# The input map of a state-space mixer as one float32r product over three stacked splits

## The chip, the cores and the metric

The kernel runs on one core of a Trainium2 chip. The metric is the device time of one execution in microseconds (us). The core's engines work side by side, each on its own list of instructions in a fixed order: TensorE (PE; its weight loads are listed as PEld), VectorE (DVE), ScalarE (ACT), GpSimd (POOL) and SyncE (SP), which here issues nearly all DMA transfers.

## The reference

A decoder of two layers over 256 positions with 2048 channels. Each layer has a hybrid mixer with four groups, a cross attention to a memory and a feed-forward network with 5632 hidden channels. The part that is changed is the input map of the first group, a state-space mixer with 32 groups of 16 channels and 64 complex states:

```python
bb_re = z_re[..., None] * b_re - z_im[..., None] * b_im
bb_im = z_re[..., None] * b_im + z_im[..., None] * b_re
bu_re = jnp.einsum('bsgc,gpc->bsgp', uf, bb_re)
bu_im = jnp.einsum('bsgc,gpc->bsgp', uf, bb_im)
...
_, _, x_re, x_im = lax.associative_scan(_s5_combine, elems, axis=1)
y = (jnp.einsum('bsgp,gcp->bsgc', x_re, c_re) - jnp.einsum('bsgp,gcp->bsgc', x_im, c_im)
     + d_skip * uf)
```

The factor `z` depends on group and state only. The recurrence between the two maps is linear with one coefficient for each group and state.

## The kernel before

Nearly all the work is products of the 256 positions with large weight matrices. Weights and activations are f32; each is split into a rounded float32r part (`whi`, `h`) and a remainder (`wlo`, `l`), and three float32r products stand for one. `load_split` brings a weight tile of 256 rows by 512 columns into one of three buffers `raw` (line 271, on SP's queue), ACT rounds it (line 272), DVE subtracts (line 273). There are four buffers for each result. Each tile then feeds twelve products of 512 columns (lines 285 to 287).

The small parts of a layer are written as generators ("lanes"). `pump`, called after each tile of a weight product, advances each lane by its rate, so their instructions are spread among the weight products. A planner then sets the order of instructions on each engine from this written order, from priorities (`load_split` stands 100 places earlier) and from when it takes operands and buffers to be ready. The order is fixed before the kernel runs.

The state-space lane has three parts. `s5_prep` runs once a layer (in layer 0 in the mixer's first block, in layer 1 during the feed-forward network before): it loads B and C, multiplies B by `z` on DVE (lines 604 to 610), transposes both on PE in sets of four (lines 613 and 626) and makes the tables `tab`. `s5_mixer` goes through four quarters `j` of four tiles `ii`. `u`, transposed to `uT`, is copied for each tile by POOL into 32 rows of `band`, whose other rows are zero (line 694), and two f32 products of 256 columns give the real and the imaginary input of the recurrence (lines 700 and 701). Some 14 DVE instructions for each tile do the recurrence (lines 704 to 723), then the output map `CT` is applied (line 730). `s5_tail` applies the gate and the norm and leaves the group's split result in `ys_h` and `ys_l`, which `w_out` needs last but one: it starts with the tiles of two other groups.

The pool `xt` (16 buffers of 4 KB a partition) holds activations, tables and maps; `k4` (7 buffers) holds attention operands.

Of the kernel before, what the change touches and what calls it, by code (L numbers as in the profile page):

```python
# [10 lines left out]
F = mybir.dt.float32  # L11
# [3 lines left out]
AF = mybir.ActivationFunctionType  # L15
OP = mybir.AluOpType
# [3 lines left out]
T = 256  # L20
D = 2048
L = 2
# [3 lines left out]
MAGIC = 12582912.0  # L26
ALPHA = (2 * L) ** 0.25
S5_RATE, CMP_RATE, NSA_RATE, SB_RATE, REST_RATE, PREP_RATE, XA_RATE = 1.05, 1.0, 0.9, 0.9, 2.0, 1.0, 1.3
N_K4, N_EV, N_S5, N_ATT, N_RAW, N_W, N_MM = 7, 3, 6, 7, 3, 4, 4
SPLIT_AHEAD = 100  # L30
FIRST_BLK = 4
N_Y4 = 1
# [6 lines left out]
TF = 128  # L39
# [2 lines left out]

_CONST_PARTS = [
    ("ident", 128), ("ropek", 128), ("ropeq", 128), ("ropec", 64), ("blk", 8), ("sel", 128),
    ("perm", 128), ("cmask", 32), ("cvalid", 2), ("mt", 256), ("ntri", 128), ("tio", TF), ("par", 2), ("sel4", 32),
]
_MASK_PARTS = [("causal", 128), ("strict", 128), ("dil", 256)]

# [1 line left out]
def _shape_consts():  # L50
    p = np.arange(128)
    c = {}
    c["ident"] = np.eye(128)
    inv = (np.float32(10000.0) ** (-np.arange(32, dtype=np.float32) / np.float32(32))).astype(np.float32)

    def tab(pos):
        a = (pos.astype(np.float32)[:, None] * inv[None, :]).astype(np.float32).astype(np.float64)
        return np.cos(a), np.sin(a)

    cs = np.zeros((128, 2, 2, 32))  # L60
    for tt in range(2):
# [24 lines left out]
    c["cmask"] = cm.reshape(128, 32)  # L86
    c["cvalid"] = cv
    d = p[:, None] + 128 - np.arange(256)[None, :]
    mt = (d >= 0) * ((d <= 128) * 1.0 + (d % 4 == 0) + (d % 16 == 0))
    c["mt"] = mt  # L90
    c["ntri"] = -1.0 * (p[:, None] >= p[None, :])
    c["tio"] = np.broadcast_to(np.arange(float(TF))[None, :], (128, TF))
    c["par"] = np.stack([(p // 16) % 2 == 0, (p // 16) % 2 == 1], 1)
    c["sel4"] = (p[:, None] % 32 == np.arange(32)[None, :])
    m = {}
    m["causal"] = np.where(p[None, :] <= p[:, None], 0.0, NEG)
    m["strict"] = np.where(p[:, None] < p[None, :], 0.0, NEG)
    m["dil"] = np.where(mt > 0, 0.0, NEG)
    f = [np.asarray(c[n], np.float32).reshape(128, w) for n, w in _CONST_PARTS]
    g = [np.asarray(m[n], np.float32).reshape(128, w) for n, w in _MASK_PARTS]  # L100
    return np.ascontiguousarray(np.concatenate(f + g, 1))


def bcast_rows(ap, n):
# [4 lines left out]
def kernel(ctx: ExitStack, tc: tile.TileContext, a: dict, cst: bass.AP, out: bass.AP,  # L109
# [3 lines left out]
    te, ve, ae, ge, sy = nc.tensor, nc.vector, nc.scalar, nc.gpsimd, nc.sync  # L113
# [22 lines left out]
    C, o = {}, 0  # L136
# [3 lines left out]
    ident = C["ident"]  # L140
# [20 lines left out]
    band = const.tile([128, 4, T], F, name="band")  # L161
    for t in (*pair, band):
        ge.memset(t, 0.0)
    turn_of_pair = [0]

# [14 lines left out]
    def ps(name="ps"):  # L180
        return psum.tile([128, 512], F, tag="ps", bufs=8 - N_MM, name=name)
# [23 lines left out]
        return wk.tile(list(shape), F, tag="y4", bufs=N_Y4, name=name)  # L205

    def xt_piece(name, shape=(128, 4, T), dt=R):
        return main.tile(list(shape), dt, tag="xt", bufs=16, name=name)

    def dump(key, ap):  # L210
        if key in dbg:
# [377 lines left out]

    def s5_prep(l, phi, zz, turn, res):  # L590

        BT = xt_piece("BT", (128, 2, 4, 128), F)
        CT = xt_piece("CT", (128, 2, 4, 128), F)
        bn = [s52([128, 16, 16], name="bn") for _ in range(2)]
        for q, n in enumerate(("s5_b_re", "s5_b_im")):
            v = a[n][l].rearrange("(i q) p c -> q p i c", q=2)
            for g in range(2):
                sy.dma_start(bn[q][g * 64:(g + 1) * 64], v[g])
        zr = zz[:, 0, l, :, None].to_broadcast([128, 16, 16])
        zi = zz[:, 1, l, :, None].to_broadcast([128, 16, 16])  # L600
        for q in range(2):
            t12 = s52([128, 2, 16, 16], name="bt")
            t1, t2 = t12[:, 0], t12[:, 1]
            ve.tensor_tensor(t1, bn[q], zr, op=OP.mult)
            ve.tensor_tensor(t2, bn[1 - q], zi, op=OP.mult)
            bx = s52([128, 16, 2, 16], name="bx")
            ge.memset(bx, 0.0)
            for g in range(2):
                s = slice(g * 64, (g + 1) * 64)
                ve.tensor_tensor(bx[s, :, g, :], t1[s], t2[s], op=OP.add if q else OP.subtract)  # L610
            pt = ps()
            for j in range(4):
                te.transpose(pt[:, j * 128:(j + 1) * 128],
                             bx[:, 4 * j:4 * j + 4].rearrange("p i q c -> p (i q c)"), ident)
            ae.activation(BT[:, q].rearrange("p j s -> p (j s)"), pt, AF.Copy)
            yield
        for q, n in enumerate(("s5_c_re", "s5_c_im")):
            cn = s52([128, 4, 64], name="cn")
            sy.dma_start(cn, a[n][l].rearrange("(j g) c p -> (g c) j p", g=8))
            ce = s52([128, 4, 2, 64], name="ce")  # L620
            for g in range(2):
                ve.tensor_scalar(ce[:, :, g, :], cn, C["par"][:, g:g + 1], -1.0 if q else 1.0,
                                 op0=OP.mult, op1=OP.mult)
            pt = ps()
            for j in range(4):
                te.transpose(pt[:, j * 128:(j + 1) * 128], ce[:, j].rearrange("p q s -> p (q s)"), ident)
            ae.activation(CT[:, q].rearrange("p j s -> p (j s)"), pt, AF.Copy)
            yield
        tabs = []
        res.update(BT=BT, CT=CT, tabs=tabs, turn=turn[l])  # L630
        for i4 in range(4):
            tb = xt_piece(f"tab{i4}", (128, 4, 2, TF), F)
            av = s52([128, 4, TF], name="ta")
            y = s52([128, 4, TF], name="ty")
            for i in range(4):
                ae.activation(y[:, i], C["tio"], AF.Copy, scale=phi[:, l, 4 * i4 + i:4 * i4 + i + 1])
            ve.tensor_scalar(av, y, MAGIC, -MAGIC, op0=OP.add, op1=OP.add)
            ve.tensor_tensor(y, y, av, op=OP.subtract)
            act(tb[:, :, 1, :], y, AF.Sin, scale=SIN_SCALE)
            ae.activation(av, y, AF.Abs)  # L640
            act(tb[:, :, 0, :], av, AF.Sin, scale=-SIN_SCALE, bias=halfpi)
            tabs.append(tb)
            yield
# [37 lines left out]
        yield  # L681

    def s5_mixer(l, u, prep, mag, out_y):
        BT, CT, tabs = prep["BT"], prep["CT"], prep["tabs"]
        uT = xt_piece("uT", dt=F)
        tcos, tsin = prep["turn"]
        for tt in range(2):
            nat_T(u[:, tt], uT, tt)
        yield
        for j in range(4):  # L690
            X = []
            for ii in range(4):
                rs = slice(ii * 32, ii * 32 + 32)
                ge.tensor_copy(band[rs, ii], uT[rs, j])
            for ii in range(4):
                i = 4 * j + ii
                tb = tabs[j][:, ii, :, None, :].to_broadcast([128, 2, 2, TF])
                fr = "p q (f t) -> p q f t"
                pb = ps("pb").rearrange("p (q t) -> p q t", q=2)
                te.matmul(pb[:, 0], BT[:, 0, j, :], band[:, ii], start=True, stop=False, skip_group_check=True)  # L700
                te.matmul(pb[:, 1], BT[:, 1, j, :], band[:, ii], start=False, stop=True, skip_group_check=True)
                A = s52([128, 2, T], name="rA")
                B = s52([128, 2, T], name="rB")
                ve.tensor_tensor(A.rearrange(fr, f=2), pb.rearrange(fr, f=2), tb, op=OP.mult)
# [586 lines left out]
    for l in range(layers):  # L1291
# [43 lines left out]
        prep_gen = None  # L1335


_INS = ["x", "mem", "ln_in_g", "ln_in_b", "w_in", "s5_lambda_re", "s5_lambda_im", "s5_log_dt", "s5_b_re", "s5_b_im",
        "s5_c_re", "s5_c_im", "s5_d", "s5_w_glu", "s5_b_glu", "nsa_cmp_pe", "nsa_cmp_w1", "nsa_cmp_w2", "mix_norm_g",
        "w_out", "ln1_g", "ln1_b", "xa_wq", "xa_wkv", "xa_wo", "ln2_g", "ln2_b", "ffn_w_gate", "ffn_w_up",  # L1340
        "ffn_w_down", "ln3_g", "ln3_b"]

# [19 lines left out]
```

## Time and profile before

| | |
|---|---|
| median of three runs | 2576.04 us (2575.46 to 2577.42) |
| the profiled execution | 2577.51 us, its span 2575.4 us |
| PE busy | 2521.7 us, 98% of the span |
| DVE busy | 1613.9 us, 63% |
| ACT busy | 1225.8 us, 48% |
| moved by DMA | 457.67 MB, 178 GB/s on average |
| granted TensorE clock | 0.998 of full speed on average |

The span runs from the first to the last instruction. Matmuls are pipelined: a record of one shows longer than the distance to the next, so this document takes distances between starts. An f32 product has two records.

### The profile page before, as it was taken

What the parts mean: (1) busy time and instruction counts of PE and PEld (TensorE: products, weight loads), DVE (VectorE), ACT (ScalarE), POOL (GpSimd) and SP (SyncE); (2) the same over time, 40 slices, a digit from 0 to 9 for tenths busy, and PEclk for the clock granted to TensorE, in tenths of its full rate; (3) what the DMA queues carried; (4) which work ended last, traced back from release to release, by engine and by line L of the source; (5) the groups of instructions that cost most, each with busy time, mean ns of one, the idle gap of its engine ahead of it and who ended that gap; (6) DMA issues with size and microseconds to landing.
All of it is one profiled execution on the core that took longest, in us unless ns stands there. A gap on an engine that the chain in (4) does not pass through costs nothing.

```text
span 2575.4 us, 32103 instructions
## 1 busy us (share of the span) xinstructions
PE 2521.7 (98%) x12019; PEld 2035.3 (79%) x12019; DVE 1613.9 (63%) x2378; ACT 1225.8 (48%) x1739; POOL 73.1 (3%) x137
## 2 busy tenths in 40 slices
PE   7999999999999999999999999999999999999997
PEld 5767778878888888888877777788788888888886
DVE  7887866676554554454679877675755555545546
ACT  3656584444434434434544567645444444344342
POOL 1000000000000000000000000100000000000000
PEclk9999999999999999999999999999999999999999
DMA  8644446556666666666656435465666666666664
GB/s 230 174 120 119 131 144 201 178 167 195 189 194 189 192 191 189 192 191 190 209 161 181 117 114 173 143 200 173 211 188 191 194 190 189 193 189 188 195 189 146
DMA packets 256027, 457.67 MB, mean 178 GB/s; under 512 B 25936, under 2 KB 38528, under 8 KB 255872
## 3 DMA queue, kind: packets, MB, share of 16 engines
q1 hardware_dynamic: 255296, 454.58, 59.6%
q8 instruction: 94, 1.54, 0.2%
q10 hardware_dynamic: 576, 1.05, 0.1%
q14 instruction: 61, 0.50, 0.1%
HBM read 453.47 MB, written 2.10 MB: 177 GB/s over the span
## 4 chain that ended last, share of the span: by engine, by line
PE 90%; DVE 5%; DMA 2%; ACT 1%; issue 1%; POOL 0%; SPq 0%; POOLq 0%; DVEq 0%; ACTq 0%
PE mm L287 25%; PE mm L285 25%; PE mm L286 25%; PE tr L377 2%; DVE wlo L273 2%; PE mm L311 1%; PE mm L313 1%; PE mm L312 1%; PE pt L813 1%; PE ns L932 1%; PE nY L946 1%; DVE H L415 1%; ACT whi L272 1%; PE pb L700 1%; PE nt L650 0%
## 5 line engine op out<-in xcount | busy, mean ns | idle before, releaser
L273 DVE TENSOR_TENSOR wlo<-raw,whi 128x1024 fp32r<-128x1024 f32 (+1 forms) x820 | 994.7, 1214 | 856.1 <-ACT whi L272 854.7
L272 ACT ACTIVATE whi<-raw 128x1024 fp32r<-128x1024 f32 (+1 forms) x820 | 862.9, 1053 | 1134.4 <-PE mm L287 998.7
L285 PE MATMUL mm<-whi,h_0h 128*128 128x512 f32 (+1 forms) x1024 | 400.3, 391 | 0.0
L286 PE MATMUL mm<-wlo,h_0h 128*128 128x512 f32 (+1 forms) x1024 | 399.1, 390 | 0.0
L287 PE MATMUL mm<-whi,h_0l 128*128 128x512 f32 (+1 forms) x1024 | 398.9, 390 | 0.0
L287 PE MATMUL mm<-whi,h_1l 128*128 128x512 f32 x720 | 281.2, 391 | 0.0
L285 PE MATMUL mm<-whi,h_1h 128*128 128x512 f32 x720 | 281.1, 390 | 0.0
L286 PE MATMUL mm<-wlo,h_1h 128*128 128x512 f32 x720 | 280.6, 390 | 0.0
L285 PE MATMUL mm<-whi,hidh 128*128 128x512 f32 x672 | 262.8, 391 | 0.0
L287 PE MATMUL mm<-whi,hidl 128*128 128x512 f32 x672 | 262.6, 391 | 0.0
L286 PE MATMUL mm<-wlo,hidh 128*128 128x512 f32 x672 | 261.7, 389 | 0.0
L285 PEld LDWEIGHTS mm<-whi,h_0h 128*128 128x128 f32 x1024 | 192.5, 188 | 40.4 <-issue 2.7
L286 PEld LDWEIGHTS mm<-wlo,h_0h 128*128 128x128 f32 x1024 | 192.5, 188 | 39.6 <-issue 2.2
L287 PEld LDWEIGHTS mm<-whi,h_0l 128*128 128x128 f32 x1024 | 192.5, 188 | 38.8 <-issue 1.4
L286 PEld LDWEIGHTS mm<-wlo,h_1h 128*128 128x128 f32 x720 | 135.3, 188 | 27.8
L285 PEld LDWEIGHTS mm<-whi,h_1h 128*128 128x128 f32 x720 | 135.2, 188 | 27.7
L287 PEld LDWEIGHTS mm<-whi,h_1l 128*128 128x128 f32 x720 | 135.3, 188 | 27.7
L286 PEld LDWEIGHTS mm<-wlo,hidh 128*128 128x128 f32 x672 | 126.3, 188 | 26.0
L287 PEld LDWEIGHTS mm<-whi,hidl 128*128 128x128 f32 x672 | 126.2, 188 | 25.9
L285 PEld LDWEIGHTS mm<-whi,hidh 128*128 128x128 f32 x672 | 126.2, 188 | 25.6
L286 PE MATMUL mm<-wlo,hinh 128*128 128x512 f32 (+1 forms) x288 | 112.1, 389 | 3.0 <-DVE wlo L273 3.0
L287 PE MATMUL mm<-whi,hinl 128*128 128x512 f32 (+1 forms) x288 | 112.0, 389 | 0.0
(379 smaller groups left out, 3097.2 us busy)
## 6 DMA issues: line engine op xcount, KB each, us to landing
raw<-in_ffn_w_gate_dram SPq DMA_DIRECT2D x176, 512.0 KB, 4.0
raw<-in_ffn_w_up_dram SPq DMA_DIRECT2D x176, 512.0 KB, 3.7
raw<-in_ffn_w_down_dram SPq DMA_DIRECT2D x176, 512.0 KB, 3.8
raw<-in_w_in_dram SPq DMA_DIRECT2D x144, 512.0 KB, 3.7
raw<-in_w_out_dram SPq DMA_DIRECT2D x64, 512.0 KB, 4.0
raw<-in_xa_wkv_dram SPq DMA_DIRECT2D x32, 512.0 KB, 4.4
raw<-in_xa_wq_dram SPq DMA_DIRECT2D x16, 512.0 KB, 4.5
raw<-in_xa_wo_dram SPq DMA_DIRECT2D x16, 512.0 KB, 4.3
```

Source lines behind the costliest of these rows:

```text
L272: ae.activation(hi[:, :k * n], raw[:, :k * n], AF.Copy)
L273: ve.tensor_tensor(lo[:, :k * n], raw[:, :k * n], hi[:, :k * n].bitcast(F), op=OP.subtract)
L285: te.matmul(P[tt][:, :n], h, hi[:, k, :], start=kk == first, stop=False)
L286: te.matmul(P[tt][:, :n], h, lo[:, k, :], start=False, stop=False)
L287: te.matmul(P[tt][:, :n], lw, hi[:, k, :], start=False, stop=kk == nk - 1)
L311: te.matmul(P[tt][:, :n], h, W[kk][0], start=kk == 0, stop=False)
L312: te.matmul(P[tt][:, :n], h, W[kk][1], start=False, stop=False)
L313: te.matmul(P[tt][:, :n], lw, W[kk][0], start=False, stop=kk == nk - 1)
L377: te.transpose(pt[:, k * 128:(k + 1) * 128], src[:, k * 128:(k + 1) * 128], ident)
L415: ve.scalar_tensor_tensor(z, z, r, G[c][1], op0=OP.mult, op1=OP.add)
L700: te.matmul(pb[:, 0], BT[:, 0, j, :], band[:, ii], start=True, stop=False, skip_group_check=True)
L813: te.transpose(pt[:, (i * nb + b) * 128:(i * nb + b + 1) * 128], p[:, i, b * 128:(b + 1) * 128], ident)
```

## The change

The host now lays out B as a block map for each layer and quarter, 96 rows by 1024 columns, with the same values three times in rows 0 to 31, 32 to 63 and 64 to 95, and C as a map for each layer. B is no longer multiplied by `z`: since the recurrence is linear and `z` is constant over positions, C is multiplied by `z` instead (six DVE instructions a layer, no transposes). In the mixer, `u` is split into `uh` and `ul`. For each quarter a raw buffer takes the map; ACT rounds all 96 rows to float32r, and DVE puts the remainder into rows 32 to 63. A second raw buffer takes twelve copies by DMA from SBUF to SBUF (four tiles; `uT`, `uT` and `ul`, 32 rows each), which ACT rounds into `U3`. One product over 96 rows then sums rounded map times rounded `u`, remainder of the map times rounded `u`, and map times remainder of `u`. There is one more step of the lane in each quarter and two fewer in the preparation. `band` goes, `xt` gets 18 buffers, `k4` six.

```diff
-N_K4, N_EV, N_S5, N_ATT, N_RAW, N_W, N_MM = 7, 3, 6, 7, 3, 4, 4
+N_K4, N_EV, N_S5, N_ATT, N_RAW, N_W, N_MM, N_XT = 6, 3, 6, 7, 3, 4, 4, 18
...
+def _s5_layouts(inputs):
+    b = np.zeros((L, 4, 3, 2, 16, 4, 2, 2, 64), np.float32)
+    c = np.zeros((L, 2, 2, 64, 16, 2, 16), np.float32)
+    for q, n in enumerate(("re", "im")):
+        bv = np.asarray(inputs["s5_b_" + n]).reshape(L, 4, 4, 2, 64, 16)
+        cv = np.asarray(inputs["s5_c_" + n]).reshape(L, 16, 2, 16, 64)
+        for g in range(2):
+            for k in range(3):
+                b[:, :, k, g, :, :, q, g, :] = bv[:, :, :, g].transpose(0, 1, 4, 2, 3)
+            c[:, q, g, :, :, g, :] = cv[:, :, g].transpose(0, 3, 1, 2)
+    return {"s5_b_map": b.reshape(L, 4, 96, 1024), "s5_c_map": c.reshape(L, 2, 128, 512)}
...
     def s5_prep(l, phi, zz, turn, res):
-        BT = xt_piece("BT", (128, 2, 4, 128), F)
         CT = xt_piece("CT", (128, 2, 4, 128), F)
...
-            ve.tensor_tensor(t1, bn[q], zr, op=OP.mult)
-            ve.tensor_tensor(t2, bn[1 - q], zi, op=OP.mult)
...
-            for j in range(4):
-                te.transpose(pt[:, j * 128:(j + 1) * 128],
-                             bx[:, 4 * j:4 * j + 4].rearrange("p i q c -> p (i q c)"), ident)
...
+        for q in range(2):
+            sy.dma_start(cn[q], a["s5_c_map"][l, q])
...
+            ve.tensor_tensor(o, fold16(cn[q]), zr, op=OP.mult)
+            ve.tensor_tensor(t, fold16(cn[1 - q]), zi, op=OP.mult)
+            if q == 0:
+                ve.tensor_tensor(o, o, t, op=OP.subtract)
+            else:
+                ve.scalar_tensor_tensor(o, o, -1.0, t, op0=OP.mult, op1=OP.subtract)
             yield
...
     def s5_mixer(l, u, prep, mag, out_y):
...
+        uh, ul = xt_piece("uTh"), xt_piece("uTl")
         for tt in range(2):
-            nat_T(u[:, tt], uT, tt)
+            pt = ps("nt")
+            for k in range(4):
+                te.transpose(pt[:, k * 128:(k + 1) * 128], u[:, tt, k * 128:(k + 1) * 128], ident)
+            pv, s = pt.rearrange("p (k t) -> p k t", k=4), slice(tt * 128, tt * 128 + 128)
+            ae.activation(uT[:, :, s], pv, AF.Copy)
+            split_evac(pv, uh[:, :, s], ul[:, :, s])
         yield
         for j in range(4):
             X = []
+            raw = wp.tile([128, 1024], F, tag="raw", bufs=N_RAW, name="raw")
+            sy.dma_start(raw[0:96], a["s5_b_map"][l, j])
+            B3 = xt_piece("B3", (128, 4, 2, 128))
+            bf = B3.rearrange("p i q s -> p (i q s)")
+            ae.activation(bf[0:96], raw[0:96], AF.Copy)
+            ve.tensor_tensor(bf[32:64], raw[32:64], bf[32:64].bitcast(F), op=OP.subtract)
+            raw = wp.tile([128, 1024], F, tag="raw", bufs=N_RAW, name="raw")
             for ii in range(4):
                 rs = slice(ii * 32, ii * 32 + 32)
-                ge.tensor_copy(band[rs, ii], uT[rs, j])
+                for k, src in enumerate((uT, uT, ul.bitcast(F))):
+                    sy.dma_start(raw[k * 32:k * 32 + 32, ii * T:ii * T + T], src[rs, j])
+            U3 = xt_piece("U3", (128, 4, T))
+            ae.activation(U3[0:96].rearrange("p i t -> p (i t)"), raw[0:96], AF.Copy)
+            yield
             for ii in range(4):
...
-                te.matmul(pb[:, 0], BT[:, 0, j, :], band[:, ii], start=True, stop=False, skip_group_check=True)
-                te.matmul(pb[:, 1], BT[:, 1, j, :], band[:, ii], start=False, stop=True, skip_group_check=True)
+                te.matmul(pb[:, 0], B3[0:96, ii, 0, :], U3[0:96, ii], start=True, stop=False, skip_group_check=True)
+                te.matmul(pb[:, 1], B3[0:96, ii, 1, :], U3[0:96, ii], start=False, stop=True, skip_group_check=True)
```

## Rows read from the trace of the kernel before

**Rows 1.** The page: busy us (share of span) x instructions; the chain by engine.

```profile
PE 2521.7 (98%) x12019; PEld 2035.3 (79%) x12019; DVE 1613.9 (63%) x2378; ACT 1225.8 (48%) x1739; POOL 73.1 (3%) x137
...
PE 90%; DVE 5%; DMA 2%; ACT 1%; issue 1%; POOL 0%; SPq 0%; POOLq 0%; DVEq 0%; ACTq 0%
```

**Rows 2.** Waits of the engines: us in total, times, longest us.

```profile
ACT whi L272 <- PE mm L287: 998.7, 646, 3.5
...
POOL band L694 <- PE pb L701: 245.9, 23, 19.6
```

**Rows 3.** Waits of the load queue SP, same columns.

```profile
SPq L271 <- DVE wlo L273: 1827.7, 729, 14.0
...
SPq L860 <- PE pc L865: 13.7, 1, 13.7
```

**Rows 4.** Table by stage: length, then busy us (x) of PE, PEld, DVE, ACT, POOL.

```profile
116.00:148.00 32.00, 28.22 (x157) 20.61 (x154) 30.79 (x87) 9.55 (x14) 1.68 (x5) 1.00 0.41 114
...
1335.00:1420.00 85.00, 83.46 (x508) 66.74 (x507) 76.96 (x197) 35.06 (x57) 6.31 (x14) 1.00 0.57 161
```

**Rows 5.** The tile `pb`: records of one product line; ns min/median/max, starts.

```profile
L700 PE MATMUL pb<-band,BT x64: 377/380/484, 97.3 to 1535.9; 128*128 128x256 f32 x64
```

**Rows 6.** Timeline of PE, layer 1, around an input product: start us, us.

```profile
1346.22 0.39 PE L286 MATMUL mm<-wlo,h_0h 128*128 128x512 f32 x1
...
1347.80 0.39 PE L287 MATMUL mm<-whi,h_0l 128*128 128x512 f32 x1
...
1349.12 0.40 PE L286 MATMUL mm<-wlo,h_0h 128*128 128x512 f32 x1
```

**Rows 7.** Timeline of PE, the gate's products, first and last of 39.

```profile
1570.18 0.28 PE L760 MATMUL mm<-gTh,whi 128*128 128x256 f32 x1
...
1574.73 0.28 PE L763 MATMUL mm<-gTl,whi 128*128 128x256 f32 x1
```

**Rows 8.** Timeline of PE around the preparation's transposes, layers 0 and 1.

```profile
70.66 0.29 PE L286 MATMUL mm<-wlo,hinh 128*128 128x280 f32 x1
70.79 0.29 PE L287 MATMUL mm<-whi,hinl 128*128 128x280 f32 x1
...
73.72 0.29 PE L287 MATMUL mm<-whi,hinl 128*128 128x280 f32 x1
...
1255.44 0.40 PE L287 MATMUL mm<-whi,hidl 128*128 128x512 f32 x1
...
1256.35 0.39 PE L286 MATMUL mm<-wlo,hidh 128*128 128x512 f32 x1
```

**Rows 9.** Groups by form: busy us, mean ns of one, idle before.

```profile
L273 DVE TENSOR_TENSOR wlo<-raw,whi 128x1024 fp32r<-128x1024 f32 x804 | 982.9, 1224 | 854.3 <-ACT whi L272 853.1
L272 ACT ACTIVATE whi<-raw 128x1024 fp32r<-128x1024 f32 x804 | 852.2, 1060 | 1119.9 <-PE mm L287 988.7 <-DMA raw<-in_w_in_dram 39.8 <-PE mm L313 18.4
...
L372 DVE TENSOR_TENSOR hidl<-tr,hidh 128x512 fp32r<-128x512 f32 x44 | 28.2, 682 | 0.0
...
L707 DVE TENSOR_TENSOR rA<-rA 128x256 f32<-128x256 f32 x32 | 13.3, 415 | 0.0
...
L610 DVE TENSOR_TENSOR bx<-bt 64x256 f32<-64x256 f32 x8 | 3.3, 417 | 0.2
```

**Rows 10.** DMA: one issue (ns min/median/max), landings of 64 KB and of `cw`, PE's wait.

```profile
L1164 SPq DMA_DIRECT2D memn<-in_mem_dram x16: 328/341/433, 317.1 to 1702.3; - x16
...
w<-in_nsa_cmp_w_dram SPq DMA_DIRECT2D x2, 64.0 KB, 2.1
...
DMA to landing us min/median/max: 3.6/5.3/6.6
...
PE ch L845 <- DMA cw<-in_nsa_cmp_w_dram: 1.7, 2, 1.0
```

**Rows 11.** Timeline, layer 1: the lane's last result on ACT, first product of `w_out`.

```profile
1604.24 0.62 ACT L371 ACTIVATE ys_h<-yn 128x512 fp32r<-128x512 f32 x1
...
1613.01 0.48 PE L285 MATMUL mm<-whi,ys_h 128*128 128x512 f32 x1
```

More of the change, by code (lines that the diff above doesn't have):

```diff
@@ L44 @@
     ("ident", 128), ("ropek", 128), ("ropeq", 128), ("ropec", 64), ("blk", 8), ("sel", 128),
-    ("perm", 128), ("cmask", 32), ("cvalid", 2), ("mt", 256), ("ntri", 128), ("tio", TF), ("par", 2), ("sel4", 32),
+    ("perm", 128), ("cmask", 32), ("cvalid", 2), ("mt", 256), ("ntri", 128), ("tio", TF), ("sel4", 32),
 ]
@@ L160 @@
     pair = [const.tile([128, 2, T], F, name=f"pair{i}") for i in range(2)]
-    band = const.tile([128, 4, T], F, name="band")
-    for t in (*pair, band):
+    for t in pair:
         ge.memset(t, 0.0)
@@ L207, in xt_piece @@
     def xt_piece(name, shape=(128, 4, T), dt=R):
-        return main.tile(list(shape), dt, tag="xt", bufs=16, name=name)
+        return main.tile(list(shape), dt, tag="xt", bufs=N_XT, name=name)
     def dump(key, ap):
@@ L590, in s5_prep @@
     def s5_prep(l, phi, zz, turn, res):
-        BT = xt_piece("BT", (128, 2, 4, 128), F)
         CT = xt_piece("CT", (128, 2, 4, 128), F)
[L594 to L600, printed above, removed]
@@ L601, in s5_prep @@
-        for q in range(2):
-            t12 = s52([128, 2, 16, 16], name="bt")
-            t1, t2 = t12[:, 0], t12[:, 1]
-            ve.tensor_tensor(t1, bn[q], zr, op=OP.mult)
-            ve.tensor_tensor(t2, bn[1 - q], zi, op=OP.mult)
[L606 to L611, printed above, removed]
-            for j in range(4):
-                te.transpose(pt[:, j * 128:(j + 1) * 128],
-                             bx[:, 4 * j:4 * j + 4].rearrange("p i q c -> p (i q c)"), ident)
-            ae.activation(BT[:, q].rearrange("p j s -> p (j s)"), pt, AF.Copy)
-            yield
@@ L617, in s5_prep @@
[L617 to L627, printed above, removed]
+        cn = [s52([128, 512], name="cn") for _ in range(2)]
@@ new lines, in s5_prep @@
+        for q in range(2):
+            sy.dma_start(cn[q], a["s5_c_map"][l, q])
+        fold16 = lambda t: t.rearrange("p (i c) -> p i c", i=16)
+        zr = zz[:, 0, l, :, None].to_broadcast([128, 16, 32])
+        zi = zz[:, 1, l, :, None].to_broadcast([128, 16, 32])
+        for q in range(2):
+            o = fold16(CT[:, q].rearrange("p j s -> p (j s)"))
+            t = fold16(s52([128, 512], name="ct"))
+            ve.tensor_tensor(o, fold16(cn[q]), zr, op=OP.mult)
[4 more added lines that the diff above has]
+                ve.scalar_tensor_tensor(o, o, -1.0, t, op0=OP.mult, op1=OP.subtract)
@@ L628, in s5_prep @@
             yield
         tabs = []
-        res.update(BT=BT, CT=CT, tabs=tabs, turn=turn[l])
+        res.update(CT=CT, tabs=tabs, turn=turn[l])
         for i4 in range(4):
@@ L683, in s5_mixer @@
     def s5_mixer(l, u, prep, mag, out_y):
-        BT, CT, tabs = prep["BT"], prep["CT"], prep["tabs"]
+        CT, tabs = prep["CT"], prep["tabs"]
         uT = xt_piece("uT", dt=F)
         tcos, tsin = prep["turn"]
+        uh, ul = xt_piece("uTh"), xt_piece("uTl")
         for tt in range(2):
-            nat_T(u[:, tt], uT, tt)
+            pt = ps("nt")
[4 more added lines that the diff above has]
+            split_evac(pv, uh[:, :, s], ul[:, :, s])
         yield
@@ L1335 @@
         prep_gen = None
-_INS = ["x", "mem", "ln_in_g", "ln_in_b", "w_in", "s5_lambda_re", "s5_lambda_im", "s5_log_dt", "s5_b_re", "s5_b_im",
-        "s5_c_re", "s5_c_im", "s5_d", "s5_w_glu", "s5_b_glu", "nsa_cmp_pe", "nsa_cmp_w1", "nsa_cmp_w2", "mix_norm_g",
+_INS = ["x", "mem", "ln_in_g", "ln_in_b", "w_in", "s5_lambda_re", "s5_lambda_im", "s5_log_dt", "s5_b_map",
+        "s5_c_map", "s5_d", "s5_w_glu", "s5_b_glu", "nsa_cmp_pe", "nsa_cmp_w1", "nsa_cmp_w2", "mix_norm_g",
         "w_out", "ln1_g", "ln1_b", "xa_wq", "xa_wkv", "xa_wo", "ln2_g", "ln2_b", "ffn_w_gate", "ffn_w_up",
@@ L1349 @@
     arrays, aps = {}, {}
+    inputs = {**inputs, **_s5_layouts(inputs)}
     for name in _INS:
```

1 line of the change is left out of this document (removed).

## The prediction

> **What bounds the kernel now.** I read the page first: TensorE (PE) is busy 98% of the span and holds 90% of the chain that ended last [rows 1]. So a microsecond saved counts if it is PE time, and a microsecond added elsewhere counts only if PE comes to wait for it. The waits say how near the others are. ScalarE's rounding copy of a weight tile (line 272) waits 998.7 us in all for PE to give a buffer back, and the VectorE (DVE) copy of the state-space lane never holds PE up: the POOL copies into `band` wait for the product, 245.9 us, not the product for them [rows 2]. The load queue (SP) spends 1827.7 us waiting for line 273 to free a raw buffer [rows 3]. Weights are therefore normally ahead of PE. The table by stage shows the exception. From 116 to 148 us DVE is busy 30.79 of 32 us and PE only 28.22; from 1335 to 1420 us DVE has 76.96 of 85 us and PE 83.46 [rows 4]. Both stretches lie at the start of the state-space lane, where this change works, and in the first DVE, not PE, sets the pace.
>
> **The products.** In layer 1 PE issues weight products of 512 columns 0.226 us apart (seven steps from 1346.22 to 1347.80). Between the starts at 1347.80 and 1349.12 lie one such step, the two products of the input map and one more step: 1.32 - 2 x 0.226 = 0.868, so 0.434 us for each f32 product of 256 columns [rows 6]. The float32r products of 256 columns in the gate of the same mixer start 4.55 us apart over 38 steps, 0.120 us each [rows 7]. The new product has that type and that width, with 96 rows instead of 128. One saves 0.434 - 0.120 = 0.314 us. Each line's 64 records [rows 5] are two for each of its 32 products (two layers, four quarters, four tiles), so there are 64 products: 64 x 0.314 = 20.1 us. Bounds: 0.120 as taken, or 0.226, the nearest larger float32r product, which would leave 64 x 0.208 = 13.3. I take 20.1, since the gate's product differs in nothing but rows.
>
> **The transposes of the preparation.** Four of them between two weight products in layer 1: 0.91 from 1255.44 to 1256.35, less two steps of 0.226, is 0.46 us. There are eight such sets (two for B and two for C per layer): 3.7 us. In layer 0 the stretch from 70.79 to 73.72 holds 2.93 us; its eight transposes (0.92) and three products of 280 columns at 0.13 (0.39) leave 1.6 us in which PE stood still for them [rows 8]. That stall goes with them, and what is late next there is nothing of this lane: the new input product needs neither `zz` nor a prepared B. Between 0 and 1.6; I take 1.6, as the products behind it ran at once.
>
> Saved in all: 20.1 + 3.7 + 1.6 = 25.4 us of PE.
>
> **What it adds to DVE and ACT.** A DVE instruction costs by its columns: 64 x 256 takes 417 ns, 128 x 256 takes 415. The subtraction that makes the low split on 32 rows of 1024 columns therefore costs what line 273 costs, 1.22 us, four times a layer; the two splits of `u` take 0.68 each. That is 4 x 1.22 + 2 x 0.68 = 6.2 us a layer. The preparation loses twelve operations (eight on 256 columns at 0.42, four near that) and gains six on 512 columns at 0.68: about nothing. ACT gets two copies of 1.06 us for each quarter and two of half the columns for `u` [rows 9]. What hides this is DVE's and ACT's free time outside the two tight stretches. In those it isn't hidden. There the PE time that the products save (two of them twice in the first, 1.25 us; fourteen in the second, 4.4 us) is worth little while DVE is full, and one to two of the new subtractions and a layer's two splits fall in. From 0 (the work moves into freer stretches) to 1.25 + 4.4 + 12.4 = 18 us; I take a third, 6 us, because PE is at 98% in the longer of the two and DVE stays below PE after it.
>
> **What it adds to the queue and the buffers.** For each quarter SP issues one map load and twelve copies of 32 KB from SBUF to SBUF, and these hold two of the three raw buffers in turn. No copy from SBUF to SBUF is in the trace. Nearest rows: 328 ns and up for an issue; 2.1 us to landing for 64 KB, up to 6.6 for the compression weights [rows 10]. So twelve issues take 12 x 0.33 = 4.0 us, the last lands 2.1 to 6.6 us later, ACT copies for 1.06: 7 to 12 us from a free raw buffer to `U3`. Behind them in the queue stand the weight loads, behind `U3`'s copy on ACT the weight roundings, behind the product on PE everything. What covers it is distance. SP was once blocked much longer, 13.7 us, by line 860 [rows 3]; PE's whole loss in that stretch was 3.78 us [rows 4], most of it with DVE full. And an operand that DMA brings straight to PE, the compression weights, cost PE 1.7 us in two waits over 16 loads [rows 10]. Per quarter the price runs from 0.1 us (their mean) to the whole chain without its cover; I take 0.7, towards their longest wait of 1.0, since twelve transfers must all land: 8 x 0.7 = 5.6 us.
>
> The Trainium skill (DMA: Bandwidth & Descriptors, Rules for kernel authors) says that many small transfers should be joined into a large one, and that under 64 KB one pays mostly overhead. That rule speaks against the twelve copies. The trace's load of 64 KB, 2.1 us to landing whatever its bytes cost, doesn't speak against it.
>
> The 16 buffers of `xt` become 18 and the seven of `k4` six. When the stick-breaking operands are made, six are in use; the next, `dqT`, comes a full block of weights (eight loads) later, so I price that at nothing. If the cover failed, it would be a wait of a few us, twice.
>
> **Sum.** 25.4 - 6 - 5.6 = 13.8 us. The profiled execution took 2577.51 us, 2.1 more than its span, and lies 1.5 above the median of 2576.04. So 2562 us on the median's scale.
>
> **Rivals.**
> *All of the saving arrives.* DVE's additions fall into free time, the copies come early: 2576.0 - 25.4 = 2551 us. For it: the subtraction and the copies don't depend on the quarter before, so they can run ahead. Against it: the two full stretches [rows 4].
> *The stacked operand comes late (slower).* One step of the lane lies between `U3`'s copy and its product, about 12 weight products / 1.05 = 2.6 us. If the order on PE leaves only that, a quarter stalls 7 - 2.6 = 4.4 to 12 - 2.6 = 9.4 us, and eight make 35 to 75: 2586 to 2626 us. This is what the rule of the Trainium skill on small transfers (DMA: Bandwidth & Descriptors) would do here. It decides from 25.4 / 8 = 3.2 us per quarter on. For it: DMA has never stood between PE and this lane before, and SP serves it in order. Against it: `band` and its product stood in the same step, without any cover by a step, and PE never waited [rows 2, 5], so the order on PE is not that in which the lane is written.
> *DVE or the weights take it back.* All 18 us fall on PE, or the queue's blocks cost in proportion to the one seen: 2576 - 25.4 + 18 + 5.6 = about 2574 us, no change.
> *The lane ends late.* Four more steps a layer, at least 4 x 2.6 = 10.4 us, and a first product that starts some 8 us later. The lane's result was ready at about 1605, `w_out` began at 1613.01 [rows 11] with four steps (48 x 0.226 = 10.8 us) that don't need it: 19 us of slack. It just holds; if it doesn't, some 5 us a layer: 2572 us.
>
> **Chances.** The forecast, some of the saving given back (2555 to 2570): 0.50. All of it (2549 to 2555): 0.24. Taken back by DVE, weights or the lane's end (2570 to 2582): 0.13. Late operand (beyond 2582): 0.13. A measurement can tell about 0.2% (5.2 us) from no change, so the bounds are 2570.9 and 2581.2. Faster 0.75; same 0.12; slower 0.13. The range, 2549 to 2584, leaves out most of the late operand and little below.
>
> **What would show it.** Products of the input map 0.12 us apart instead of 0.434; no transposes at 72 and 1255 us; PE busy some 24 us less in sum; PE's waits before the input product under 1 us each. Waits of several us on PE before it, or on ACT before `U3`'s copy with PE idle behind them, would show the late operand. PE idle beside a full DVE in the two tight stretches [rows 4] would show DVE or the weights taking it back; a wait of `w_out` for the lane's group the fourth.

## The result and the profile after

The changed kernel takes 2597.59 us (median of 4 runs, 2592.84 to 2598.89) where the kernel before took 2576.73 beside it: ratio 1.0077, 95% interval [1.0061, 1.0093], about 21 us slower. The forecast was 2562 us, with a range that ended at 2584. The profile below is that of the fastest of the four executions, 2592.84 us.

The page of the changed kernel, the two rows that answer to [rows 1]. Line numbers are always those of the kernel that a row is from: the weight loads, rounding, subtraction and products of lines 271, 272, 273 and 285 to 287 stand in lines 285, 286, 287 and 299 to 301 of the changed kernel.

```profile
PE 2513.5 (97%) x11923; PEld 2022.0 (78%) x11923; DVE 1622.5 (63%) x2378; ACT 1240.5 (48%) x1751; POOL 52.1 (2%) x100
...
PE 85%; DVE 7%; DMA 4%; ACT 3%; issue 1%; SPq 1%; POOL 0%; POOLq 0%; DVEq 0%; ACTq 0%
```

PE has 96 instructions fewer, as it should (64 records of float32 products and 32 transposes), but its share of the chain fell from 90 to 85%, and DMA and ACT hold 7% of it instead of 3%. PE's busy time fell by 8.2 us and not by the 24 that were named as a sign. In this execution the granted clock was 0.992 on average instead of 0.998, and 0.006 of 2513.5 us is an estimated 15 us of slower products. Something now makes PE wait. The products themselves are what was forecast. Timeline of PE around the first input product of layer 0, start and length in us:

```profile
102.46 0.28 PE L712 MATMUL pb<-U,B 96*128 96x256 f32 x1
102.58 0.28 PE L713 MATMUL pb<-U,B 96*128 96x256 f32 x1
102.70 0.27 PE L1084 MATMUL kt<-call,krope 128*128 128x128 f32 x1
```

They start 0.12 us apart, against 0.434 before [rows 6], and PE does not wait for them. Where it does wait is seen in its timeline, in three rows, two of layer 0 and one of layer 1, with the idle time before the instruction and what ended it in brackets:

```profile
84.74 1.93 PE L857 MATMUL ch<-cw,cA 128*32 128x128 f32 x32 [4.76 <-DVE cA L849]
92.39 0.83 PE L299 MATMUL mm<-whi,hinh 128*128 128x280 f32 x2 [5.72 <-ACT whi L286]
...
1343.32 1.22 PE L299 MATMUL mm<-whi,h_0h 128*128 128x512 f32 x2 [4.20 <-ACT whi L286]
```

The two rows of line 299 stand at a weight product, at the start of the lane's first quarter. The wait for `cA`, an operand of another group, lies in the same gap of layer 0, and first_quarter_pool below is without it. The waits of SP's queue in these two stretches (78 to 130 and 1300 to 1640 us) name what is new in front of the weights:

```profile
SPq L703 <- ACT uTh L385: 14.7, 1, 14.7
...
SPq L703 <- ACT uTh L385: 11.0, 1, 11.0
```

Line 703 is the line of the twelve copies that stack `u`. In each layer SP stood still once, at the first of them, until ScalarE had brought the transposed `u` out. The rows name `uTh` (line 385), but the first copy reads `uT`, which ScalarE writes in the same step (line 687). It started as the second half of `uT` was done, at 87.51, while `uTh` ran on to 87.99:

```profile
86.92 0.59 ACT L687 ACTIVATE uT<-nt 128x512 f32<-128x512 f32 x1
...
87.54 0.56 SPq L703 DMA_DIRECT2D raw<-uT  x1
```

The expectations and the text below call this step the split of `u`. The chain that ended last, taken from 74 to 104 us, shows what follows (start us, us):

```profile
85.93 0.61 ACT tab L245
86.54 0.48 ACT uTh L385
...
88.03 0.60 DVE uTl L386
88.63 3.02 DMA raw<-in_w_in_dram
91.67 0.68 ACT whi L286
92.39 0.83 PE mm L299 x2
```

Read it backwards. PE waits for a rounded weight tile, ScalarE for that tile's load, and the load was issued only at 88.63, behind the first copy. In layer 0 the step that makes `uT` and `uTh` stands among the preparation's tables on ScalarE (line 245); in layer 1 ScalarE waits for PE's transposes of `u` until 1335.97. The table by stage shows the hole, then the price (columns as in [rows 4]; after the five engines come the granted clock, the DMA share and GB/s):

```profile
80.00:88.00 8.00, 1.93 (x32) 1.51 (x32) 2.83 (x7) 6.84 (x17) 0.15 (x1) 0.67 0.01 2
88.00:96.00 8.00, 3.61 (x14) 3.34 (x15) 3.39 (x4) 2.43 (x4) 0.00 (x0) 0.50 0.52 142
80.00:120.00 40.00, 27.54 (x153) 22.41 (x154) 26.64 (x58) 21.89 (x41) 0.15 (x1) 0.83 0.55 161
...
1340.00:1350.00 10.00, 6.64 (x17) 4.79 (x18) 2.97 (x4) 3.17 (x3) 0.00 (x0) 0.66 0.77 230
1340.00:1380.00 40.00, 34.18 (x214) 27.86 (x215) 28.93 (x64) 16.46 (x26) 0.16 (x1) 0.91 0.69 199
```

The same two stretches of 40 us in the kernel before:

```profile
80.00:120.00 40.00, 38.02 (x250) 29.97 (x248) 31.83 (x75) 27.92 (x55) 3.74 (x7) 1.00 0.74 216
...
1340.00:1380.00 40.00, 38.49 (x248) 32.46 (x248) 37.17 (x91) 16.89 (x35) 2.62 (x6) 1.00 0.62 176
```

From 80 to 88 us the DMA share is 0.01: hardly any transfer is under way. After the wait PE runs at a granted clock of 0.50, its 1.2 GHz level, so a wait is paid for twice, once as idle time and once in slow products.

### The profile page after: what moved, and what is told of

Its sections match the earlier page's. It is cut to its first block, busy times and chain, and to the rows that moved or that the text cites. A ratio compares the mean times of both kernels' runs of the same rounds, so it can differ in the third digit from the quotient of the medians.

```text
span 2591.1 us, 31964 instructions
## 1 busy us (share of the span) xinstructions
PE 2513.5 (97%) x11923; PEld 2022.0 (78%) x11923; DVE 1622.5 (63%) x2378; ACT 1240.5 (48%) x1751; POOL 52.1 (2%) x100
## 4 chain that ended last, share of the span: by engine, by line
PE 85%; DVE 7%; DMA 4%; ACT 3%; issue 1%; SPq 1%; POOL 0%; POOLq 0%; DVEq 0%; ACTq 0%
PE mm L300 25%; PE mm L301 24%; PE mm L299 24%; DVE wlo L287 2%; DMA raw<-in_w_in_dram 2%; PE tr L391 2%; ACT whi L286 1%; PE mm L325 1%; PE mm L327 1%; PE pt L825 1%; PE mm L326 1%; DVE H L429 1%; PE nY L958 1%; PE ns L944 1%; DMA cw<-in_nsa_cmp_w_dram 0%
## 5 line engine op out<-in xcount | busy, mean ns | idle before, releaser
L299 PE MATMUL mm<-whi,hinh 128*128 128x512 f32 (+1 forms) x288 | 112.1, 395 | 8.2 <-ACT whi L286 8.2
```

The source lines that it names most:

```text
L299: te.matmul(P[tt][:, :n], h, hi[:, k, :], start=kk == first, stop=False)
```

## The experiments

Seventeen kernels were run. Times are medians in us; the kernel before, run beside them, took 2576.5 to 2577.4. Theory A in the expectations is that SP's queue stands behind the split of `u` in each layer's first quarter. Theory B is that the twelve issues and the raw buffer cost alike in every quarter. C lays the loss on VectorE's added work or the lane's end, D on VectorE's added work, E on the lane's added steps and its late end.

### Who copies `u`, and when

**pool_copies**: POOL copies the split of `u` into the stack; no copy by DMA, no raw buffer for it. The map's load and everything else stay.

```
-  raw = wp.tile(...)
-  sy.dma_start(raw[k*32:k*32+32, ii*T:ii*T+T], src[rs, j])     # src: uT, uT, ul
-  ae.activation(U3[0:96]..., raw[0:96], AF.Copy)
+  ge.tensor_copy(U3[k*32:k*32+32, ii], src[rs, j])             # src: uh, uh, ul
```

> The stacked operand is written by 12 POOL copies per quarter, out of the split of u, with no DMA, no raw buffer and no ACT copy for it; all else as in the changed kernel. If the queue (its wait or its issues) is the loss, the saving of PE comes through: 2555 to 2568 us. If DVE's added work or the lane's late end is the loss, it stays at 2588 or more.

Measured: 2580.17, ratio 1.0012 [1.0003, 1.0022]. 17.4 us of the loss are gone with the copies on SP; the whole of the forecast gain is still missing.

**first_quarter_pool** does this in the first quarter of each layer alone (`if j == 0`), **later_quarters_pool** in the other three alone (`if j > 0`).

> Only the first quarter of each layer is written by POOL copies, the other three as in the changed kernel. Theory A (the SP queue stands behind the split of u, 14.7 and 11.0 us, at each layer's first quarter, and weights run out): 2572 to 2580 us, most of the loss gone. Theory B (every quarter's twelve issues and its raw buffer cost alike): a quarter of the loss gone, 2588 to 2592 us. Theory C (DVE, lane's end): no change, 2595 us.

> The first quarter as in the changed kernel, the other three by POOL copies. Theory A: 2582 to 2592 us, most of the loss stays. Theory B: 2566 to 2572 us, three quarters of the loss gone. Theory C: 2595 us.

Measured: 2577.96, ratio 1.0005 [0.9995, 1.0014], and 2597.35, ratio 1.0082 [1.0067, 1.0097]. This settles the place. 24 of the 96 copies carry the whole loss by the queue; the other 72 cost no more on SP than on POOL. (What they would cost against no copies at all, no run shows.) Two rows of the table by stage of first_quarter_pool, for the stretches shown above:

```profile
80.00:120.00 40.00, 34.33 (x194) 25.78 (x193) 34.28 (x80) 24.93 (x45) 7.74 (x13) 0.96 0.72 209
...
1340.00:1380.00 40.00, 38.69 (x268) 31.34 (x267) 38.10 (x100) 18.40 (x36) 0.16 (x1) 1.00 0.63 183
```

Add to the idle time what the missing clock makes of the busy time. In the first stretch the changed kernel loses 12.46 + 27.54 x 0.17 = 17.1 us, this one 5.67 + 34.33 x 0.04 = 7.0. In the second it is 5.82 + 34.18 x 0.09 = 8.9 against 1.3. The differences, 10.1 and 7.6, make 17.7 us; the two profiled executions lie 2592.8 - 2576.7 = 16.2 apart, and the medians 2597.6 - 2578.0 = 19.6. So the waits of these two stretches are enough for this loss.

The products at the end of each layer (line 325, before 311) show it a second way. Their first start lies at the end of layer 0 and their last at the end of layer 1; the rows are of the kernel before, the changed one and first_quarter_pool:

```profile
L311 PE MATMUL mm<-whi,hidh x32: 387/389/390, 1287.5 to 2561.4; 128*128 128x512 f32 x32
...
L325 PE MATMUL mm<-whi,hidh x32: 389/389/393, 1287.4 to 2577.2; 128*128 128x512 f32 x32
...
L325 PE MATMUL mm<-whi,hidh x32: 387/389/390, 1279.4 to 2561.0; 128*128 128x512 f32 x32
```

The changed kernel and first_quarter_pool lie 8.0 us apart after layer 0 and 16.2 at the end. In these executions the changed kernel ends layer 0 level with the kernel before, since the queue's loss there takes back the gain, and its whole loss stands in layer 1. In later_quarters_pool the waits of SP for the split stand as in the changed kernel, 14.7 and 11.0 us.

The Trainium skill (DMA: Bandwidth & Descriptors, Anatomy of one DMA — SWDGE (gpsimd) path) states that DMA engines don't wait on semaphores: the wait happens on the sequencer that issues, before dispatch. The trace agrees: while SP waited 14.7 us, it issued none of the loads that stand behind the copy, and the DMA share fell to 0.01. The Trainium skill (DMA: Bandwidth & Descriptors, Rules for kernel authors) warns of many small transfers. That rule does not tell this case, since the 72 copies of the later quarters are as small and cost no more than POOL's.

**copies_on_pool_queue**: the twelve copies stay DMA transfers into a raw buffer, but are issued on POOL's queue.

```
-  sy.dma_start(raw[k*32:k*32+32, ii*T:ii*T+T], src[rs, j])
+  ge.dma_start(raw[k*32:k*32+32, ii*T:ii*T+T], src[rs, j])
```

> The same twelve transfers and raw buffers as in the changed kernel, but issued by POOL's queue, so that no weight load stands behind them. If the place in SP's queue is the loss (A or B): 2560 to 2575 us. If it is the raw buffers that the map and the copies hold: 2588 us or more.

Measured: 2588.83, ratio 1.0050 [1.0034, 1.0067]: half. SP no longer waits for the split, but one of its waits from 78 to 130 us is new:

```profile
SPq L285 <- DVE B L698: 13.5, 1, 13.5
```

Line 285 is a weight load. It waits for the raw buffer that the map holds until its remainder is made, and ScalarE rounds the map only after it has split `u` (line 697 starts at 88.53 there, behind the last line 385 at 88.05). Of three raw buffers the map and the stack hold two. In pool_copies, where the map alone holds one, the same wait is 2.2 us. So a free queue was worth half here, and the buffers held as long are the likely other half; no run frees them alone.

### Where the forecast gain went

**pool_copies_no_step** and **pool_copies_rate** take two suspects out of pool_copies: the added step of the lane in each quarter, and the lane's speed.

```
# pool_copies_no_step: between the stack and its products
-  yield
# pool_copies_rate
-  S5_RATE = 1.05
+  S5_RATE = 1.2
```

> POOL copies as in pool_copies, and the step of the lane that the change added in each quarter taken out. Theory E (the lane ends late because it has more steps, and the work at the end of the mixer piles up on DVE): 2565 to 2573 us. Theory D (DVE's added subtractions): no change against pool_copies, 2577 to 2582 us.

> POOL copies as in pool_copies, and layer 1's lane advanced at 1.2 steps per weight tile instead of 1.05. Theory E: 2565 to 2573 us. Theory D: 2577 to 2582 us or above, since the same DVE work then comes in a shorter time.

Measured: 2576.53, ratio 0.9998 [0.9988, 1.0007], and 2579.79, ratio 1.0012 [1.0002, 1.0021]. The added step costs 3.6 us; the faster lane gains nothing.

The traces show one wait that comes and goes with the step, at the lane's end. Waits of PE in layer 1 (1300 to 1640 us), for an operand of the stick-breaking mixer, in the changed kernel and in pool_copies:

```profile
PE sz L986 <- DVE ssp L984: 3.9, 1, 3.9
...
PE sz L984 <- DVE ssp L982: 2.9, 1, 2.9
```

In the changed kernel it stands just ahead of the state-space gate's products, whose work ScalarE and VectorE do in turn with that mixer's. The kernel before and pool_copies_no_step have no such wait. pool_copies_rate hasn't either, but there PE waits 5.4 us in layer 1 for the remainders of weights (line 287), against 1.1 in pool_copies, so that its equal time does not clear the lane's end.

**pool_copies_pool_subtracts** moves the remainders of B and of `u` from VectorE to POOL (`ve.tensor_tensor` becomes `ge.tensor_tensor`).

> POOL copies as in pool_copies, and the subtractions for the map's remainder and for u's remainder moved from DVE to POOL: DVE has no work that the kernel before didn't have. Theory D: 2565 to 2572 us. Theory E: 2577 to 2583 us.

Measured: 2594.73, ratio 1.0069 [1.0054, 1.0084]. The run says nothing on VectorE: POOL takes 2666 ns for a subtraction of B's remainder where VectorE takes 1215, and PE now waits for it. (The rest of the 14.6 us above pool_copies was not followed.) Its POOL group, and a wait of PE from 80 to 160 us:

```profile
L699 POOL TENSOR_TENSOR B<-raw,B 32x1024 fp32r<-32x1024 f32 x8 | 21.3, 2666 | 9.8 <-ACT B L698 9.6
...
PE pb L711 <- POOL B L699: 3.7, 1, 3.7
```

**prep_only** is the change without its new product: both maps laid out by the host, the factor in the output map, but `band`, one B map for the layer and float32 products as before.

```
+  BT = xt_piece("BT", (128, 2, 4, 128), F)
+  sy.dma_start(BT..., a["s5_b_map"][l])          # host's map, 128 x 1024
...
   ge.tensor_copy(band[rs, ii], uT[rs, j])        # products as in the kernel before
```

> The kernel before with only the preparation changed: the host lays out B (loaded as it stands) and C, the factor goes into the output map, no transposes; band and the f32 products stay. By the prediction's term the transposes and their stall give 5.3 us: 2570 to 2573 us. If other work takes up what the front of a layer saves, no change, 2575 to 2578 us.

Measured: 2570.16, ratio 0.9975 [0.9966, 0.9984], 6.6 us below the kernel before. With prep_fewer_slots below, which takes as long, it is the fastest kernel of the study that computes all that the reference asks for.

**rounded_only** goes on from there with float32r products, rounded B and rounded `u`, and leaves the remainders out of the computation. **prep_fewer_slots** is prep_only with six instead of seven `k4` buffers (and 17 of `xt`).

```
# rounded_only
-  BT = xt_piece("BT", (128, 2, 4, 128), F);  band = const.tile([128, 4, T], F)
+  BT = xt_piece("BT", (128, 2, 4, 128));     band = const.tile([128, 4, T], R)
+  ae.activation(BT[:, q]..., b0, AF.Copy)
```

> This kernel is the one with the host's map, the factor in the output map, `band` and BT of before (2570.2 us), with BT and `band` in float32r, so that the 64 products take 0.12 us instead of 0.434. It leaves out part of the computation: the remainders of B and of u, so there is no stack, no copy of u by DMA, no subtraction and no map per quarter. Theory P (the stretches that hold the products are paced by PE, and the saving is lost only to what the change added beside it): the whole 64 x 0.314 = 20 us arrives, 2550 us (2546 to 2555). Theory D (in these stretches VectorE or the weights arrive as late as PE does, so a shorter product only makes PE wait): less than half of it arrives, 2560 to 2570 us.

> The kernel prep_only (2570.2 us, float32 products) with 6 instead of 7 tiles in the pool that the change cut from 7 to 6. If the smaller pool costs part of what was lost: 3 to 10 us above 2570. If not: 2569 to 2572.

Measured: 2563.25, ratio 0.9943 [0.9927, 0.9960], and 2570.12, ratio 0.9970 [0.9958, 0.9982]. Of the 20.1 us of PE time that the products save, 6.9 arrive. The buffers cost nothing.

The sum of PE's busy time over thirteen stretches of 40 us (80 to 360 and 1340 to 1580 us, those that hold the products), with two of the stretches, first of prep_only:

```profile
120.00:160.00 40.00, 39.19 (x210) 29.97 (x210) 38.88 (x97) 17.34 (x29) 1.67 (x4) 1.00 0.51 148
...
1460.00:1500.00 40.00, 39.86 (x212) 29.17 (x211) 34.37 (x79) 23.24 (x50) 0.40 (x1) 1.00 0.40 119
...
sum 520.00, PE 514.46 PEld 387.43 DVE 432.05 ACT 309.66 POOL 29.94; mean PE 39.57 PEld 29.80 DVE 33.23 ACT 23.82 POOL 2.30
```

And of rounded_only:

```profile
120.00:160.00 40.00, 36.02 (x196) 27.22 (x189) 36.77 (x89) 13.83 (x19) 1.28 (x4) 0.91 0.52 146
...
1460.00:1500.00 40.00, 38.13 (x197) 26.93 (x196) 32.19 (x75) 22.03 (x48) 0.40 (x1) 0.96 0.40 118
...
sum 520.00, PE 505.97 PEld 378.76 DVE 432.07 ACT 312.37 POOL 28.49; mean PE 38.92 PEld 29.14 DVE 33.24 ACT 24.03 POOL 2.19
```

PE is idle 514.46 - 505.97 = 8.5 us more, and the clock below 1.00 in these two stretches is worth 36.02 x 0.09 + 38.13 x 0.04 = 4.8: 13.3 us, about the 13.2 that are missing. (The stretches are fixed while the faster kernel runs up to 6 us ahead, so this is an estimate.) One of the waits, in PE's timeline of rounded_only:

```profile
132.63 0.38 PE L865 MATMUL pc<-w,chs 128*15 128x64 f32 x4 [3.55 <-DVE chs L660]
...
136.48 0.63 PE L301 MATMUL mm<-wlo,hinh 128*128 128x512 f32 x1
136.90 0.63 PE L302 MATMUL mm<-whi,hinl 128*128 128x512 f32 x1
```

and what VectorE did meanwhile:

```profile
130.77 0.68 DVE L720 TENSOR_TENSOR rA<-rz,tab 128x512 f32<-128x512 f32 x1
131.37 0.68 DVE L721 TENSOR_TENSOR rB<-rz,tab 128x512 f32<-128x512 f32 x1
131.97 0.42 DVE L722 TENSOR_TENSOR rA<-rA 128x256 f32<-128x256 f32 x1
132.30 0.18 DVE L660 SCALAR_TENSOR_TENSOR chs<-gl,chs 128x32 f32<-128x32 f32 x1
```

VectorE goes through the recurrence and other work without a gap and comes to `chs` at 132.30; PE has waited 3.55 us for it, and afterwards its weight products start 0.42 us apart instead of 0.23. In prep_only there is no such wait from 80 to 160 us.

That could still be the planner's doing, since it writes the order anew for shorter products. **rounded_two_products** and **rounded_three_products** give PE time back in equal steps: each tile's first product is done three or five times, each over the last.

```
-  te.matmul(pb[:, 0], BT[:, 0, j, :], band[:, ii], start=True, ...)
+  for _ in range(3):                    # 5 in rounded_three_products
+      te.matmul(pb[:, 0], BT[:, 0, j, :], band[:, ii], start=True, ...)
```

> The kernel rounded_only (2563.3 us, remainders of B and u left out) with 64 more products: each tile's first input product is done three times, each over the last, so nothing else changes. That gives TensorE back 64 x 0.12 = 7.7 us of the 20.1 us that float32r had saved. If TensorE's time in these stretches is worth a third (as 7 of 20 us suggested): 2566 us (2564 to 2568). If it is worth its whole length, and the missing 13 us of rounded_only are only the order that the planner wrote with the shorter products: 2571 us, or an irregular value, since each kernel's order is planned anew.

> As rounded_two_products with 128 more products (each tile's first input product five times, each over the last; remainders of B and u left out): 15.4 us of TensorE given back. A third of it: 2568 to 2570 us. All of it: 2579 us. If the two kernels don't lie on one line with rounded_only (0, 7.7 and 15.4 us added), the planner's order counts for as much as the products.

Measured: 2563.52, ratio 0.9948 [0.9933, 0.9963], and 2564.89, ratio 0.9952 [0.9936, 0.9969]. 15.4 us of added PE time raise the median by 1.6 us (2.3 by the ratios), less than any of the expectations allowed. The three intervals overlap; they rule out that the added time counts in full, not that a third of it does. The sums over the same thirteen stretches tell why, here of rounded_three_products:

```profile
sum 520.00, PE 511.54 PEld 389.07 DVE 435.85 ACT 313.48 POOL 27.46; mean PE 39.35 PEld 29.93 DVE 33.53 ACT 24.11 POOL 2.11
```

The added products fill time in which PE had been idle (505.97, then 511.54), the wait for `chs` shrinks from 3.6 us to two of 0.7 together, and the clock is 1.00 in all thirteen. Where another engine holds the lane up, added PE time is nearly free; it doesn't follow that saved time is worth as little, since 6.9 of 20.1 us did arrive.

### What the added work beside the products costs

These kernels put parts of the change back into rounded_only, as work whose results nobody reads.

```
# rounded_plus_subtracts: per half of u, and twice per quarter
+  ve.tensor_tensor(dm, v, v, op=OP.subtract)               # 128 x 512; 32 x 512
# rounded_plus_map: per quarter
+  sy.dma_start(raw[0:96], a["s5_b_map"][l, 0:96]);  ae.activation(raw[0:96], raw[0:96], AF.Copy)
# rounded_plus_copies: per tile, two more
+  ge.tensor_copy(dc[0:32, k*T:k*T+T], uT[rs, j])
```

> The kernel rounded_only (remainders of B and u left out) with the VectorE work of the change put back as work whose results nobody reads: one 128x512 subtraction for each half of u and two 32x512 subtractions for each quarter, about 10 x 0.68 = 6.8 us in each layer by the row of a 128x512 operation. Theory P: VectorE's work is covered, within 3 us of rounded_only. Theory D (VectorE sets the pace of the lane): 8 to 14 us above rounded_only.

> The kernel rounded_only (remainders of B and u left out) with the map's load put back as work whose result nobody reads: in each quarter one 96x1024 load into a raw slot of the weights, on SP's queue, and its rounding by ScalarE. It waits for nothing but the slot. If the raw slots and SP's transfers are what takes the gain back in the kernel with the copies on GpSimd: 6 to 15 us above rounded_only. If only the copies of u, which wait for a result, cost anything there: within 3 us of it.

> The kernel rounded_only (2563.3 us, remainders of B and u left out) with GpSimd's copies brought from 4 to the 12 of pool_copies in each quarter: 8 more of 32x256, about 8 x 0.5 = 4 us of GpSimd in each quarter ahead of its last products, into a tile that nobody reads. If the chain of copies ahead of the products is the rest of what pool_copies lost (2580.2 - 2570.1 = 10 us): 7 to 12 us above rounded_only. If GpSimd's work is covered: within 3 us of it.

> The kernel rounded_only (remainders of B and u left out) with both added as work whose results nobody reads: the subtractions on VectorE of rounded_plus_subtracts and GpSimd's 8 more copies a quarter. If these two are the whole difference to pool_copies: 2577 to 2582 us. If copies are covered and only VectorE counts: 2569 to 2573, and the rest of the 10 us sits in what these kernels don't hold (the copies that round u twice over, the stack's slots, the added step of the lane).

Measured: 2570.13, ratio 0.9969 [0.9959, 0.9979]; 2562.66, ratio 0.9940 [0.9925, 0.9955]; 2566.66, ratio 0.9960 [0.9945, 0.9975]; 2573.89, ratio 0.9988 [0.9979, 0.9998]. So the subtractions cost 6.9 us, the map's load and rounding nothing, POOL's copies 3.4 (their interval overlaps that of rounded_only), and both together 10.6, close to the sum.

**pool_copies_no_subtracts** checks the largest of these in the change itself: pool_copies with three rounded copies of `u` and the rounded map three times, so the remainders are left out.

```
-  split_evac(pv, uh[:, :, s], ul[:, :, s])
+  ae.activation(uh[:, :, s], pv, AF.Copy)
-  ve.tensor_tensor(bf[32:64], raw[32:64], bf[32:64].bitcast(F), op=OP.subtract)
```

> The kernel pool_copies (2580.2 us) without the change's subtractions: the stack holds three rounded copies of u and the map's rounded rows three times, so the remainders of u and of B are left out of the computation. Loads, rounding, copies, products and steps of the lane stay. If VectorE's added work costs in the change what it cost beside rounded_only (2570.1 - 2563.3 = 6.9 us): 2573 us (2571 to 2576). If it costs nothing there, because the copies arrive later than it: 2579 to 2581.

Measured: 2573.49, ratio 0.9985 [0.9975, 0.9994]: 6.7 us below pool_copies. VectorE's added work costs the same in both places.

## Why the prediction was wrong, point by point

The medians make one account from 2576.7 us to 2597.6, forecast beside what was measured:

| Step | forecast | measured | from |
|---|---|---|---|
| transposes and the stall gone, with the rest of the preparation's change | -5.3 | -6.6 | prep_only |
| products in float32r | -20.1 | -6.9 | rounded_only |
| VectorE's subtractions | +6 | +6.9 | rounded_plus_subtracts |
| stack: POOL's copies beside them | | +3.8 | rounded_plus_both |
| stack: the lane's step and the rest | | +6.3 | pool_copies |
| stack: copies on SP instead of POOL | | +17.4 | changed kernel |
| the three stack rows together | +5.6 | +27.5 | |

By this table forecast and measurement lie 34.7 us apart: 21.9 of them in the stack, 13.2 in what the products are worth, and the other rows nearly cancel.

*The step that failed* is "What it adds to the queue and the buffers". It priced a quarter at 0.7 us, saying "What covers it is distance". It worked the chain out from the moment a raw buffer is free (7 to 12 us) and forgot that the copies also wait for their source. In the first quarter of each layer SP comes to them before `u` is transposed and split; SP stands still for 14.7 and 11.0 us with every weight load behind it. The evidence taken for cheapness, the block of 13.7 us by line 860 [rows 3] in a stretch where PE lost only 3.78 us [rows 4], was one block at one place. Here a block of 11.0 us cost about 8 in a stretch of 40 us, and one of 14.7 about 10, and both dropped the clock. Why that earlier block was cheaper was not tried; one difference is that the map and the stack now hold two of the three raw buffers, and in copies_on_pool_queue, with these held and the queue free, about half of the loss stayed.

*The rival "The stacked operand comes late (slower)"* had the right sign and the wrong place. It looked for PE waiting before the input product; the changed kernel shows no such wait. The transfer that came late was the weights' behind it in the queue. Its time, 2586 to 2626 us, holds the result, but not by its mechanism: it asked for a stall in each of eight quarters, and the two first ones made the whole loss by the queue.

*The products* were right in themselves (0.12 us apart) and wrong in what they are worth. The prediction said that a microsecond of PE time counts because PE is busy 98% of the span, and allowed for tight stretches with 5.65 us of lost value inside the sum of 18. The page's share is a mean over the span; in the stretches of the lane another engine ends last, and 13.2 of 20.1 us came back as PE's idle time and lower clock. That VectorE is that engine is shown for one wait (3.55 us for `chs`) and by the subtractions' price; for the other waits it is argued. By the repeated products PE's time there is worth a tenth to a seventh (1.6 or 2.3 of 15.4 us); why float32 to float32r is worth more, 6.9 of 20.1, stays open. The planner's new order may be the reason. So may slack that is used up: the median is 2564.9 with 15.4 us given back and 2570.2 with all 20.1, in prep_only. No run tells the two apart.

*VectorE's added work* was sized right: 6 forecast, 6.9 and 6.7 measured. Part of that is luck, since the 6 was a third of an upper bound of 18, and no run shows that it falls in the two stretches from which the bound was made. *The transposes* and the rest of the preparation's change gave 6.6 where 5.3 were forecast for transposes and stall. *`xt` and `k4`* cost nothing, as said. *The lane's end*, the rival "The lane ends late", did cost something, though it was priced at nothing. Its named sign is there, but small: `w_out` waits 1.0 us for the lane's result, in layer 0 alone. The larger wait is the one for `ssp` in layer 1, 3.9 us in the changed kernel, which comes and goes with the lane's added step.

*A misreading* that changed nothing: the prediction gives the copies into `band` to VectorE; the row is POOL's [rows 2].

Of the last 6.3 us of the stack, 3.6 are the added step (pool_copies_no_step), likely by the wait at the lane's end; the remaining 2.7 have no cause shown and are near what these medians can tell.

## What to carry to other kernels

A copy that waits long for a result doesn't belong on the queue that loads the weights: before costing its bytes, ask when its source is ready and what is written behind it. A page that shows PE at 98% doesn't make every PE microsecond worth one; read the stage, and test a doubtful saving by giving the time back as repeated work, which takes one line. The part of this change that only removes work (host's maps, factor in the output map) was worth 0.9975 alone; the product's new form cost more on VectorE, POOL and SP than it freed.

## What the runs showed of the hardware beyond that

An issue of a copy from SBUF to SBUF on 32 partitions takes SP longer than the 328 ns from which the forecast was made [rows 10]. The source lines of the copies in the changed kernel (ns min/median/max), their landing in us, and the subtraction of 32 rows on VectorE:

```profile
L703 SPq DMA_DIRECT2D raw<-uT x64: 507/588/1195, 87.5 to 1499.6; - x64
...
DMA to landing us min/median/max: 1.8/2.3/5.0
...
L698 DVE TENSOR_TENSOR B<-raw,B 32x1024 fp32r<-32x1024 f32 x8 | 9.7, 1215 | 0.7 <-ACT B L697 0.5
```

Twelve issues are 7.1 us of SP, not 4.0, though 72 of the 96 cost no more than POOL's copies in their place. A subtraction of 32 rows costs VectorE 1215 ns, that of 128 rows 1224 [rows 9], and POOL 2666 for the same 32 rows.
